# Partial sums of the last block's up stage: kept in PSUM and seeded by ScalarE copies, instead of kept in SBUF and added by VectorE

## The chip, the cores and the metric

The kernel runs as one program on one core of a Trainium2 chip. Its time is the device time of an execution in microseconds (us). The profile is of one execution on the same kind of core; its rows count from the first instruction. PE is TensorE's matmul pipeline, PEld its weight loads, DVE is VectorE, ACT is ScalarE, POOL is GpSimd, and SP issues most of the DMAs.

## What is computed

One layer of a hybrid encoder (chunk attention and a matrix memory side by side, then a feed-forward network) is run on 2048 prompt rows and 8 x 16 sample rows. The change lies in the feed-forward part:

```
def conv_ffn(h, buf, w_up, w_conv, b_conv, w_down):
    u = h @ w_up                       # 1024 -> 2 * 2816 columns
    ext = concatenate([buf, u], axis=1)
    y = b_conv
    for j in range(CONV_W):            # width 3, along the rows of time
        y = y + ext[:, j:j + S] * w_conv[j]
    gate, up = split(y, 2, axis=-1)
    return (gelu(gate, approximate=True) * up) @ w_down, ext[:, S:]
```

Everything is float32.

## The kernel before

**Blocks and stages.** The 17 tiles of 128 rows are worked off in three blocks (FBLOCKS). Each block has an up stage (h @ w_up, convolution, gate) and a down stage. The last block (b = 2) holds tiles 12 to 15 and the sample tile; its half is n = 320 columns wide (HALF), and its up stage is what the change touches. The up stage has 22 steps, one for each 128 columns of the gate half and of the up half; in block 2 they go in the order 0, 11, 1, 12, 2, 13, ... (ORDERS).

**Seven products for eight.** In each step, a 2 x 2 product of blocks is formed by a Strassen-Winograd scheme with seven products P1 to P7. The B tiles hold the seven combinations of h, made earlier; the weights hold seven combinations of w_up, four of which (`wsd`) were stored in DRAM by block 0. Each product is four contraction tiles of 128, and each float32 product is made of three fp32r matmuls (mm3, L104 to L106: high by high, low by high, high by low), so a product is 12 matmuls of 320 columns, and a step 84.

**Weights.** load_quads issues a step's weights from SP in two groups, of four quads and of three, each quad 128 x 512 floats (256 KB). load_up splits each into a high part (ACT, L1309) and a low part (DVE, L1310) in one of two `wh`/`wl` buffers or of the four `w3` tiles.

**A step's PSUM and its sums.** `a` (ua, 2 buffers), `d_` (ub, 2 buffers) and `ec` (uec, 2 buffers of two banks: e and c). Before the change a step is:

- P1 into a; ACT copies it to x1 in SBUF (L1617).
- P6 into d_; DVE makes x2 = x1 + d_ (L1619).
- P7 into e; DVE makes x3 = x2 + e (L1621).
- P5 into c; DVE makes the second half of uu = x3 + c, in three pieces of 128, 64 and 128 columns (second, L1483).
- P2 onto a; ACT copies a into the first half of ug (L1640).
- P4 onto e; DVE makes the first half of uu = x2 + e (L1642).
- P3 onto c; DVE makes the second half of ug = x2 + c, three pieces (L1483).

"Onto" means that the matmuls accumulate on what the bank holds. uu and ug rotate through three buffers (u_tile). Then conv runs for uu and for ug: small POOL copies of the two carried rows (L1494 to L1499), a scaled ACT pass (L1502), two DVE passes (L1503, L1504), and for ug the GELU on ACT (L1506). DVE multiplies gate by up (L1652, L1655), forms four combinations every second step (L1595) and POOL stores them.

**Other work in the stage.** Twelve units finish block 1's output beside it (later): SP loads f0d or f1d and x2d, DVE scales (L1431), POOL adds (L1432) and stores.

**What sets the order.** The program is written as a list of operations and a scheduler with a timeline model orders the instructions of each engine when the program is built. That order is then fixed: each engine runs its own list from top to bottom, and an instruction that waits on a semaphore holds up all behind it on its engine.

Of the kernel before, what the change touches and what calls it, by code (L numbers as in the profile page):

```python
# [10 lines left out]
F32 = mybir.dt.float32  # L11
F32R = mybir.dt.float32r
AF = mybir.ActivationFunctionType
ALU = mybir.AluOpType
# [3 lines left out]
P = 128  # L18
# [21 lines left out]
PAIRS = [[(((b[j], 0), (b[j + 3], 0)), j * P, P, f"{b[j]}") for j in range(3)] for b in FBLOCKS[:2]]  # L40
NK = NF // 2
FAST = (1, 2)
ORDERS = [[f for k in range(NK) for f in (k, k + NK)] if b in FAST else list(range(NF)) for b in range(3)]
B11, B12, B22, B21 = range(4)
T1, T3, T2, T4 = range(4, 8)
# [4 lines left out]
def hymba_step(ctx: ExitStack, tc: tile.TileContext, I: dict, O: dict):  # L50
    nc = tc.nc
# [20 lines left out]
    def dt_(shape, name):  # L72
        return dram.tile(shape, F32, tag=name, name=name)
# [28 lines left out]
    def mm3(out, ah, al, bh, bl, start, stop, onto=False):  # L102

        nc.tensor.matmul(out, ah, bh, start=start, stop=False, skip_group_check=onto)  # L104
        nc.tensor.matmul(out, ah, bl, start=False, stop=False, skip_group_check=onto)  # L105
        nc.tensor.matmul(out, al, bh, start=False, stop=stop, skip_group_check=onto)  # L106
# [938 lines left out]
    P1, P6, P7, P5, P2, P4, P3 = range(7)  # L1045
# [13 lines left out]
    def quad(name):  # L1059
        return ffn.p3.tile([P, 512], F32, tag="q", name=name, bufs=11)  # L1060
# [184 lines left out]
    for n_, (half, gi) in enumerate(seq):  # L1245
        wh, wl, _ = pend
# [4 lines left out]
        g = GROUPS[gi]  # L1251
        i = int(g[2])
        nm = f"{g}_{half}"
# [60 lines left out]
    def load_quads(b, f, g):  # L1314

        src = lambda i: I["w_up"][f][:, i * 512:(i + 1) * 512]
        if b == 0 and g == 0:
            q = []
            for i in range(4):
                q.append(quad(f"wu{f}_{i}"))  # L1320
                nc.sync.dma_start(q[i], src(i))
            a11, a12, a22, a21 = q
            s1, s2, s3, s4 = [quad(f"ws{f}_{i}") for i in range(4)]
            for o, x, y, op in ((s1, a21, a22, ALU.add), (s2, s1, a11, ALU.subtract), (s3, a11, a21, ALU.subtract),
                                (s4, a12, s2, ALU.subtract)):
                nc.vector.tensor_tensor(o, x, y, op=op)
            for i, o in enumerate((s2, s3, s1, s4)):
                nc.gpsimd.dma_start(wsd[f][:, i * 512:(i + 1) * 512], o)
            raws[f] = [a12, a22, s4]
            return [a11, s2, s3, s1]  # L1330
        if b == 0:
            return raws.pop(f)
        kept = lambda i: wsd[f][:, i * 512:(i + 1) * 512]
        out = []
        for i, s_ in enumerate([[src(0), kept(0), kept(1), kept(2)], [src(1), src(2), kept(3)]][g]):
            r = quad(f"wu{b}_{f}_{g}_{i}")
            nc.sync.dma_start(r, s_)
            out.append(r)
        return out

    def load_up(b, i, g, quads=None):
        f = ORDERS[b][i]
        n = 2 * i + g
# [102 lines left out]
    p4 = ffn.p4 = ctx.enter_context(tc.tile_pool(name="p4", bufs=1, side="right", reuse_waits="tile"))  # L1446
# [13 lines left out]
    def u_tile(name):  # L1460
        turns[0] += 1
        if turns[0] % 3:
            return rows_tile("xr", [P, D], name)[:, :770]
        return p4.tile([P, 770], F32, tag="u", name=name)

    for b, tiles in enumerate(FBLOCKS):
        last = b == len(FBLOCKS) - 1
        fast = b in FAST
        nt = len(tiles)
        n = HALF[b]  # L1470
# [4 lines left out]
        def product(i, w, acc, onto=False):  # L1475
            for k in range(4):
                c = slice(k * P, (k + 1) * P)
                mm3(acc[:, :n], w[0][:, c], w[1][:, c], B[i][:, 0, k, :n], B[i][:, 1, k, :n],
                    start=not onto and k == 0, stop=k == 3, onto=onto)

        def second(u, x, acc):

            add = lambda o, c, v=lambda t: t: nc.vector.tensor_tensor(o, v(x[:, c]), v(acc[:, c]), op=ALU.add)  # L1483
            if not last:
                add(u[:, 2 + n:2 + 2 * n], slice(0, n))
                return
            add(u[:, 2 + n + 64:2 + n + 192], slice(0, P))
            add(u[:, 2 + n:2 + n + 64], slice(2 * P, n))
            us = u[:, 2 + npr:2 + ln].rearrange("p (b s) -> p b s", b=DB)
            add(us[:, :, 2:DS + 2], slice(P, 2 * P), lambda t: t.rearrange("p (b s) -> p b s", b=DB))  # L1490
# [24 lines left out]
        g, parts = {}, {}  # L1515
# [84 lines left out]
        unfinished = []  # L1600
        for fi, f in enumerate(ORDERS[b]):
            w = pend.pop(0)
            ahead_of(2 * fi + 2)
            if fi >= 3:
                next(done, None)
            if fi == NF - 2:
                for i in range(2):
                    if fast:
                        fetch_a(i)
                    else:  # L1610
                        fetch(0, i, True)
            nm = f"{b}_{f}"
            a, d_, ec = ps_mm(f"ua{nm}"), ps_sm(f"ub{nm}"), ps_big(f"uec{nm}")
            e, c = ec[:, 0:512], ec[:, 512:1024]
            x1, x2, x3 = [p4.tile([P, 384], F32, tag="x", name=f"x{i}_{nm}", bufs=3) for i in range(3)]
            product(P1, w[0], a)
            nc.scalar.copy(x1[:, :n], a[:, :n])  # L1617
            product(P6, w[1], d_)
            nc.vector.tensor_tensor(x2[:, :n], x1[:, :n], d_[:, :n], op=ALU.add)  # L1619
            product(P7, w[2], e)  # L1620
            nc.vector.tensor_tensor(x3[:, :n], x2[:, :n], e[:, :n], op=ALU.add)  # L1621
            product(P5, w[3], c)
            uu = u_tile(f"uu{nm}")
            second(uu, x3, c)
            w = pend.pop(0)
            ahead_of(2 * fi + 3)
            if fi == NF - 1:
                if fast:
                    split_a(0)
                    split_a(1)  # L1630
                    for i in range(2, 5):
                        fetch_a(i)
                else:
                    split_g(0, 0, w3_tile)
                    split_g(0, 1, w3_tile)
                    for k in range(2, 5):
                        fetch(0, k, True)
            ug = u_tile(f"ug{nm}")
            product(P2, w[0], a, onto=True)
            nc.scalar.copy(ug[:, 2:2 + n], a[:, :n])  # L1640
            product(P4, w[1], e, onto=True)
            nc.vector.tensor_tensor(uu[:, 2:2 + n], x2[:, :n], e[:, :n], op=ALU.add)  # L1642
            product(P3, w[2], c, onto=True)
            second(ug, x2, c)
# [21 lines left out]
        if fast:  # L1666
# [73 lines left out]
            kept = {}  # L1740
# [22 lines left out]
            for p, (_, _, set_, onto) in enumerate(SEQUENCE):  # L1763
                for c in range(3):
# [19 lines left out]
                    for k in range(4 * c, min(4 * c + 4, NK)):  # L1784
                        i = 6 * p + k // 2
# [198 lines left out]
```

## Time and profile before

| what | value |
|---|---|
| runs of the kernel | 2768.33, 2776.52, 2780.66 us; median 2776.52 |
| profiled execution | 2780.55 us, its span 2778.8 us, 1.75 us outside the span |
| granted TensorE clock | 0.994 of full, mean |
| last block's up stage | 2338.5 to 2634.5 us of the span, 296 us |
| PE instructions in that stretch | 1890 matmuls (1848 of the stage, the rest of the neighbouring down stages) |

The stretch begins where the first `ua` matmul of 320 columns stands in the timeline (2338.5 us) and ends with the last `uec` matmul (2634.1 us). Busy times overlap a little where instructions are pipelined: a matmul of 320 columns is shown as 0.31 us long, while one starts every 0.147 us. For a busy PE the count of matmuls in a stretch therefore tells more than the busy time.

### The profile page before, as it was taken

What the parts mean: (1) busy time and instruction counts of PE and PEld (TensorE: products, weight loads), DVE (VectorE), ACT (ScalarE), POOL (GpSimd) and SP (SyncE); (2) the same over time, 40 slices, a digit from 0 to 9 for tenths busy, and PEclk for the clock granted to TensorE, in tenths of its full rate; (3) what the DMA queues carried; (4) which work ended last, traced back from release to release, by engine and by line L of the source; (5) the groups of instructions that cost most, each with busy time, mean ns of one, the idle gap of its engine ahead of it and who ended that gap; (6) DMA issues with size and microseconds to landing.
All of it is one profiled execution on the core that took longest, in us unless ns stands there. A gap on an engine that the chain in (4) does not pass through costs nothing.

```text
span 2778.8 us, 47788 instructions
## 1 busy us (share of the span) xinstructions
PE 2700.5 (97%) x16422; PEld 2525.1 (91%) x16422; DVE 1971.7 (71%) x3637; ACT 1439.6 (52%) x2918; POOL 658.6 (24%) x1249
## 2 busy tenths in 40 slices
PE   7999999999999999999999999999999999999998
PEld 7899999998899998878999998789999778989976
DVE  5244455645546668766989987668998866999966
ACT  4355555634346666543555455445455665545554
POOL 1000010211100002335433322123442112555301
PEclk9999999999999999999999999999999999999999
DMA  5534355556564456345645559866775766777775
GB/s 182 157 116 139 105 164 168 163 152 211 156 184 141 136 169 196 107 163 195 230 153 188 167 183 329 301 224 198 225 225 170 250 223 231 216 236 231 233 268 183
DMA packets 322850, 532.52 MB, mean 192 GB/s; under 512 B 59650, under 2 KB 156638, under 8 KB 322478
## 3 DMA queue, kind: packets, MB, share of 16 engines
q1 hardware_dynamic: 251838, 400.11, 46.6%
q0 software_dynamic: 25840, 83.98, 7.9%
q10 hardware_dynamic: 44928, 45.37, 5.0%
q8 instruction: 129, 2.11, 0.3%
q14 instruction: 115, 0.94, 0.1%
HBM read 383.28 MB, written 149.18 MB: 192 GB/s over the span
## 4 chain that ended last, share of the span: by engine, by line
PE 49%; DVE 5%; DMA 3%; issue 2%; ACT 1%; POOL 1%; SPq 0%; DVEq 0%; POOLq 0%; ACTq 0%
PE uec L104 5%; PE uec L105 5%; PE uec L106 5%; PE dn L106 4%; PE dn L105 3%; PE dn L104 3%; PE ua L106 3%; PE ua L105 3%; PE ua L104 3%; PE wo L106 2%; PE wo L104 2%; PE wo L105 2%; PE dnm L105 1%; PE dnm L106 1%; PE dnm L104 1%
## 5 line engine op out<-in xcount | busy, mean ns | idle before, releaser
L104 PE MATMUL uec<-B,wuh 128*128 128x384 f32 (+1 forms) x720 | 237.8, 331 | 11.8 <-DVE uu L1642 10.7
L105 PE MATMUL uec<-B,wuh 128*128 128x384 f32 (+1 forms) x720 | 236.5, 328 | 0.0
L106 PE MATMUL uec<-B,wul 128*128 128x384 f32 (+1 forms) x720 | 234.8, 328 | 0.0
L1309 ACT CAST wuh<-wu 128x512 fp32r<-128x512 f32 x255 | 141.4, 618 | 112.4 <-PE uec L105 105.4
L1310 DVE TENSOR_TENSOR wul<-wu,wuh 128x512 fp32r<-128x512 f32 x255 | 170.4, 703 | 4.0 <-DMA x2d<-mx 2.8
L405 DVE CUSTOM_DVE_ANT_0 tmp<-s,nb 128x640 f32<-128x640 f32 (+4 forms) x128 | 94.4, 738 | 95.6 <-PE s L395 94.2
L104 PE MATMUL vo<-wi_h,hT 128*128 128x256 f32 x544 | 155.2, 285 | 0.8 <-DVE mt L211 0.6
L106 PE MATMUL vo<-wi_h,hT 128*128 128x256 f32 x544 | 155.6, 286 | 0.0
L105 PE MATMUL vo<-wi_l,hT 128*128 128x256 f32 x544 | 154.8, 285 | 0.0
L104 PEld LDWEIGHTS uec<-B,wuh 128*128 128x128 f32 x720 | 136.2, 189 | 15.3 <-DVE uu L1642 12.4
L104 PE MATMUL qk<-hT,wi_h 128*128 128x384 f32 (+1 forms) x384 | 130.3, 339 | 7.4 <-ACT qk_st L236 4.1
L105 PEld LDWEIGHTS uec<-B,wuh 128*128 128x128 f32 x720 | 136.4, 189 | 0.2
L106 PEld LDWEIGHTS uec<-B,wul 128*128 128x128 f32 x720 | 136.2, 189 | 0.0
L1506 ACT ACTIVATE y<-y 128x768 f32<-128x768 f32 (+1 forms) x66 | 53.8, 815 | 155.5 <-DVE y L1504 155.5
L418 DVE TENSOR_TENSOR ptl<-pt,pth 128x640 fp32r<-128x640 f32 (+4 forms) x128 | 93.7, 738 | 56.5 <-ACT pth L417 55.5
L406 ACT ACTIVATE tmp<-tmp,mn 128x640 f32<-128x640 f32 (+4 forms) x128 | 97.6, 762 | 64.2 <-DVE mn L405 62.4
L1310 DVE TENSOR_TENSOR wdl<-wdr,wdh 128x512 fp32r<-128x512 f32 x198 | 124.9, 686 | 7.0 <-ACT wdh L1309 6.8
L105 PE MATMUL qk<-hT,wi_h 128*128 128x384 f32 (+1 forms) x384 | 128.9, 336 | 0.0
L106 PE MATMUL qk<-hT,wi_l 128*128 128x384 f32 (+1 forms) x384 | 128.5, 335 | 0.0
L1310 DVE TENSOR_TENSOR al<-ar,ah 128x768 fp32r<-128x768 f32 (+2 forms) x94 | 71.1, 765 | 80.9 <-ACT ah L1309 80.7
L105 PE MATMUL qb<-hT,wi_h 128*128 128x384 f32 (+1 forms) x384 | 127.9, 333 | 0.0
L106 PE MATMUL qb<-hT,wi_l 128*128 128x384 f32 (+1 forms) x384 | 127.2, 331 | 0.0
(443 smaller groups left out, 9443.9 us busy)
## 6 DMA issues: line engine op xcount, KB each, us to landing
wu<-in_w_up SPq DMA_DIRECT2D x220, 256.0 KB, 4.4
wu<-wsd SPq DMA_DIRECT2D x176, 256.0 KB, 4.1
wdr<-in_w_down SPq DMA_DIRECT2D x110, 256.0 KB, 5.8
wi_raw<-in_w_in SPq DMA_DIRECT2D x52, 512.0 KB, 4.0
wsd<-ws POOLq DMA_DIRECT2D x88, 256.0 KB, 3.7
wdr<-wtd SPq DMA_DIRECT2D x88, 256.0 KB, 4.8
gr<-gd SPq DMA_DIRECT2D x39, 384.0 KB, 5.9
kraw<-kTd SPq DMA_DIRECT2D x112, 128.0 KB, 3.2
```

The costliest lines, as they stand in the source:

```text
L104: nc.tensor.matmul(out, ah, bh, start=start, stop=False, skip_group_check=onto)
L105: nc.tensor.matmul(out, ah, bl, start=False, stop=False, skip_group_check=onto)
L106: nc.tensor.matmul(out, al, bh, start=False, stop=stop, skip_group_check=onto)
L405: nc.vector.tensor_tensor_reduce(o_, s_, b_, 1.0, 3e38, ALU.add, ALU.min, accum_out=mn)
L406: nc.scalar.activation(tmp[:, :n], tmp[:, :n], AF.Exp, bias=mn, scale=-1.0, accum_out=rsum[:, i % 4, hh:hh + 1])
L418: nc.vector.tensor_tensor(s.ptl[:, sl, qc], ptv, s.pth[:, sl, qc], op=ALU.subtract)
L1309: nc.scalar.copy(h, r)
L1310: nc.vector.tensor_tensor(l, r, h, op=ALU.subtract)
L1506: nc.scalar.activation(y[:, :ln], y[:, :ln], AF.Gelu_apprx_tanh)
```

## The change

Only steps of block 2 (SEEDED) are touched; blocks 0 and 1 take the old path. The products of a step now go P1, P7, P6, P2, then P5, P4, P3, and the weights are loaded in that order. The partial sums stay in PSUM: ACT copies a (= P1) into d_, which is now one bank of ec, P6 accumulates onto d_, ACT copies d_ into c, the other bank of ec, and P5, P4 and P3 accumulate onto c, d_ and c. P7 goes into the ub bank and is copied by ACT to SBUF (p7). DVE is left with uu = p7 + c and uu = p7 + d_; the second half of ug is three ACT copies out of c. The buffer for ug is taken before the one for uu.

```diff
+SEEDED = (2,)
...
+        groups = [[src(0), kept(0), kept(1), kept(2)], [src(1), src(2), kept(3)]]
+        if b in SEEDED:
+            groups = [[src(0), kept(1), kept(0), src(1)], [kept(2), src(2), kept(3)]]
...
+            def add(o, c, v=lambda t: t):
+                if x is None:
+                    nc.scalar.copy(o, v(acc[:, c]))
+                else:
+                    nc.vector.tensor_tensor(o, v(x[:, c]), v(acc[:, c]), op=ALU.add)
...
+            a, sm_, ec = ps_mm(f"ua{nm}"), ps_sm(f"ub{nm}"), ps_big(f"uec{nm}")
+            seeded = b in SEEDED
+            xs = [p4.tile([P, 384], F32, tag="x", name=f"x{i}_{nm}", bufs=3) for i in range(1 if seeded else 3)]
+            if seeded:
+                d_, c, e, p7 = ec[:, 0:512], ec[:, 512:1024], sm_, xs[0]
+                product(P1, w[0], a)
+                nc.scalar.copy(d_[:, :n], a[:, :n])
+                product(P7, w[1], e)
+                nc.scalar.copy(p7[:, :n], e[:, :n])
+                product(P6, w[2], d_, onto=True)
+                nc.scalar.copy(c[:, :n], d_[:, :n])
+                product(P2, w[3], a, onto=True)
+                ug, uu = u_tile(f"ug{nm}"), u_tile(f"uu{nm}")
+                nc.scalar.copy(ug[:, 2:2 + n], a[:, :n])
...
+            if seeded:
+                product(P5, w[0], c, onto=True)
+                second(uu, p7, c)
+                product(P4, w[1], d_, onto=True)
+                nc.vector.tensor_tensor(uu[:, 2:2 + n], p7[:, :n], d_[:, :n], op=ALU.add)
+                product(P3, w[2], c, onto=True)
+                second(ug, None, c)
```

The scheduler orders the whole stage anew. Up to the stage the order on every engine is as before. In the rows below, the number behind a tile's name is its step (x_2_4, uec_4: step 4), behind it stands the buffer; uec is d_ and c, ub is P7's bank, wuh/wul are weight parts, y_f_0 belongs to ug and y_f_1 to uu.

On ACT, around step 4, before:

```order
L1502 ACTIVATE y_3_0_27622<-ug_3_27568,wcv 128x656
L1309 CAST wu_4_1_1_27719<-wu_4_1_2_27726 128x512
L1640 COPY ug_14_27734<-ua_14_27657 128x320
L1617 COPY x_2_4_27839<-ua_4_27836 128x320
L1506 ACTIVATE y_3_0_27622<-y_3_0_27622 128x656
L1502 ACTIVATE y_14_1_27780<-uu_14_27714,wcv 128x656
L1309 CAST wuh_15_0_27811<-wu_15_0_0_27813 128x512
```

And on ACT at the same place in the changed kernel (its lines are 1 to 11 higher there):

```order
L1511 ACTIVATE y_3_0_27608<-ug_3_27536,wcv 128x656
L1628 COPY uec_4_27822<-ua_4_27820 128x320
L1630 COPY x_2_4_27823<-ub_4_27821 128x320
L1515 ACTIVATE y_3_0_27608<-y_3_0_27608 128x656
L1632 COPY uec_4_27822<-uec_4_27822 128x320
L1310 CAST wuh_15_0_27795<-wu_15_0_0_27797 128x512
L1310 CAST wuh_15_0_27795<-wu_15_0_1_27799 128x512
L1310 CAST wuh_15_0_27795<-wu_15_0_2_27801 128x512
L1310 CAST wuh_15_0_27795<-wu_15_0_3_27803 128x512
L1635 COPY ug_4_27875<-ua_4_27820 128x320
```

The one copy x1 has become three: the seed of d_ (L1628), the copy of P7 (L1630) and the seed of c (L1632), with step 3's GELU (L1515) ahead of the last of them.

On DVE, around the same steps, before:

```order
L1503 SCALAR_TENSOR_TENSOR y_3_0_27622<-ug_3_27568,wcv,y_3_0_27622 128x656
L1310 TENSOR_TENSOR wu_4_1_3_27721<-wu_4_1_2_27726,wu_4_1_1_27719 128x512
L1619 TENSOR_TENSOR x_2_4_27840<-x_2_4_27839,ub_4_27837 128x320
L1504 SCALAR_TENSOR_TENSOR y_3_0_27622<-ug_3_27568,wcv,y_3_0_27622 128x656
L1621 TENSOR_TENSOR x_2_4_27841<-x_2_4_27840,uec_4_27838 128x320
L1652 TENSOR_TENSOR g_3_27627<-y_3_0_27622,y_3_1_27614 128x2x256
L1655 TENSOR_TENSOR g_3_27627<-y_3_0_27622,y_3_1_27614 128x128
L1595 TENSOR_TENSOR s_2_3_27799<-g_3_27627 128x256
L1642 TENSOR_TENSOR uu_14_27714<-x_2_14_27661,uec_14_27659 128x320
```

And on DVE in the changed kernel:

```order
L1512 SCALAR_TENSOR_TENSOR y_3_0_27608<-ug_3_27536,wcv,y_3_0_27608 128x656
L1513 SCALAR_TENSOR_TENSOR y_3_0_27608<-ug_3_27536,wcv,y_3_0_27608 128x656
L1491 TENSOR_TENSOR uu_14_27699<-x_2_14_27646,uec_14_27645 128x128
L1491 TENSOR_TENSOR uu_14_27699<-x_2_14_27646,uec_14_27645 128x64
L1491 TENSOR_TENSOR uu_14_27699<-x_2_14_27646,uec_14_27645 128x8x16
L1683 TENSOR_TENSOR g_3_27613<-y_3_0_27608,y_3_1_27600 128x2x256
L1686 TENSOR_TENSOR g_3_27613<-y_3_0_27608,y_3_1_27600 128x128
L1604 TENSOR_TENSOR s_2_3_27783<-g_3_27613 128x256
L1311 TENSOR_TENSOR wul_15_0_27796<-wu_15_0_0_27797,wuh_15_0_27795 128x512
L1311 TENSOR_TENSOR wul_15_0_27796<-wu_15_0_1_27799,wuh_15_0_27795 128x512
L1311 TENSOR_TENSOR wul_15_0_27796<-wu_15_0_2_27801,wuh_15_0_27795 128x512
L1665 TENSOR_TENSOR uu_14_27699<-x_2_14_27646,uec_14_27645 128x320
```

The sums x2 and x3 between the two passes of y_3_0 are gone, and so are the three sums for ug further down; the two passes stand next to each other. On PE the 84 matmuls of a step are the same in number and size; in step 4 the program has 2 of P1 and 2 of P7, then the other 10 of P1, 10 of P7, 12 of P6 and 12 of P2 in a row, then P4 of step 14 and P5 of step 4.

More of the change, by code (lines that the diff above doesn't have):

```diff
@@ L1334, in load_quads @@
         out = []
-        for i, s_ in enumerate([[src(0), kept(0), kept(1), kept(2)], [src(1), src(2), kept(3)]][g]):
+        groups = [[src(0), kept(0), kept(1), kept(2)], [src(1), src(2), kept(3)]]
+        if b in SEEDED:
+            groups = [[src(0), kept(1), kept(0), src(1)], [kept(2), src(2), kept(3)]]
+        for i, s_ in enumerate(groups[g]):
             r = quad(f"wu{b}_{f}_{g}_{i}")
@@ L1481, in second @@
         def second(u, x, acc):
-            add = lambda o, c, v=lambda t: t: nc.vector.tensor_tensor(o, v(x[:, c]), v(acc[:, c]), op=ALU.add)
+            def add(o, c, v=lambda t: t):
[3 more added lines that the diff above has]
+                    nc.vector.tensor_tensor(o, v(x[:, c]), v(acc[:, c]), op=ALU.add)
             if not last:
@@ L1612, in hymba_step @@
             nm = f"{b}_{f}"
[L1613 to L1624, printed above, removed]
+            a, sm_, ec = ps_mm(f"ua{nm}"), ps_sm(f"ub{nm}"), ps_big(f"uec{nm}")
[12 more added lines that the diff above has]
+                nc.scalar.copy(ug[:, 2:2 + n], a[:, :n])
+            else:
+                d_, e, c = sm_, ec[:, 0:512], ec[:, 512:1024]
+                x1, x2, x3 = xs
+                product(P1, w[0], a)
+                nc.scalar.copy(x1[:, :n], a[:, :n])
+                product(P6, w[1], d_)
+                nc.vector.tensor_tensor(x2[:, :n], x1[:, :n], d_[:, :n], op=ALU.add)
+                product(P7, w[2], e)
+                nc.vector.tensor_tensor(x3[:, :n], x2[:, :n], e[:, :n], op=ALU.add)
+                product(P5, w[3], c)
+                uu = u_tile(f"uu{nm}")
+                second(uu, x3, c)
             w = pend.pop(0)
@@ L1637, in hymba_step @@
                         fetch(0, k, True)
[L1638 to L1644, printed above, removed]
+            if seeded:
[5 more added lines that the diff above has]
+                second(ug, None, c)
+            else:
+                ug = u_tile(f"ug{nm}")
+                product(P2, w[0], a, onto=True)
+                nc.scalar.copy(ug[:, 2:2 + n], a[:, :n])
+                product(P4, w[1], e, onto=True)
+                nc.vector.tensor_tensor(uu[:, 2:2 + n], x2[:, :n], e[:, :n], op=ALU.add)
+                product(P3, w[2], c, onto=True)
+                second(ug, x2, c)
             yu = conv(uu, 1, f)
```

## The prediction

> **What bounds the kernel now.** I read the page's busy shares first, then the stretches of the last block's up stage, then who waited for whom in it, then the PE timeline around the longest wait.
>
> ```profile
> PE 2700.5 (97%) x16422; PEld 2525.1 (91%) x16422; DVE 1971.7 (71%) x3637; ACT 1439.6 (52%) x2918; POOL 658.6 (24%) x1249
> ```
>
> Over the whole span PE is busy 97% and DVE only 71%. That average hides the stage that the change touches:
>
> ```profile
> core 0: us, PE busy (x) PEld busy (x) DVE busy (x) ACT busy (x) POOL busy (x), PEclk, DMA share, GB/s
> 2338.50:2634.50 296.00, 285.88 (x1890) 281.94 (x1888) 269.94 (x539) 158.67 (x280) 149.22 (x296) 0.98 0.70 227
> 2350.00:2400.00 50.00, 50.00 (x343) 50.00 (x342) 44.52 (x93) 29.02 (x50) 18.77 (x42) 1.00 0.60 187
> 2400.00:2450.00 50.00, 47.66 (x320) 46.66 (x319) 46.48 (x94) 24.58 (x42) 31.86 (x55) 1.00 0.77 240
> 2450.00:2500.00 50.00, 45.77 (x298) 45.50 (x297) 46.64 (x89) 25.69 (x46) 29.09 (x53) 0.93 0.69 221
> 2500.00:2550.00 50.00, 48.56 (x332) 48.30 (x331) 49.98 (x99) 27.54 (x48) 28.80 (x57) 1.00 0.75 246
> 2550.00:2600.00 50.00, 47.89 (x317) 47.63 (x316) 46.21 (x97) 25.44 (x44) 24.39 (x53) 0.97 0.61 200
> ```
>
> Here DVE is busy 91%, and in the four later windows 46.2 to 49.98 of 50 us. The count of matmuls tells what this costs. The first window has 343, PE at its densest, with DVE busy 44.52 us: so DVE at 89% did not hold PE up. The next four have 320, 298, 332 and 317, together 105 too few; at 50 / 343 = 0.146 us each, that is **15.3 us lost**. Over the stage, 1848 matmuls at 0.147 us are 271.7 us, the other 42 some 7 us (most are wider), so at most 296 - 278.7 = 17.3 us can be had at all.
>
> ```profile
> PE uec L104 <- DVE uu L1642: 9.7, 4, 4.2
> ACT y L1506 <- DVE y L1504: 57.6, 17, 6.2
> ACT wuh L1309 <- PE uec L105: 25.7, 18, 3.4
> ```
>
> PE waited only for DVE: four times, 9.7 us in all, the longest 4.2. The other 5 us or so are in the clock after two of these waits:
>
> ```profile
> 2471.25 0.31 PE L106 MATMUL ua<-B,wul 128*128 128x320 f32 x1
> 2475.80 0.64 PE L104 MATMUL uec<-B,wuh 128*128 128x320 f32 x1 [4.23 <-DVE uu L1642]
> 2476.23 0.47 PE L105 MATMUL uec<-B,wuh 128*128 128x320 f32 x1
> 2476.50 0.47 PE L106 MATMUL uec<-B,wul 128*128 128x320 f32 x1
> ...
> 2555.88 0.64 PE L104 MATMUL uec<-B,wuh 128*128 128x320 f32 x1 [2.11 <-DVE uu L1642]
> 2556.31 0.47 PE L105 MATMUL uec<-B,wuh 128*128 128x320 f32 x1
> 2556.58 0.47 PE L106 MATMUL uec<-B,wul 128*128 128x320 f32 x1
> ```
>
> After 4.23 us of waiting, and again after 2.11 us, matmuls start 0.27 us apart instead of 0.147; that is the granted clock of 0.93 and 0.97 in these windows. So a wait of 2 us costs more than itself. (The Trainium skill, "TensorE: Matmul & The Clock Gate", section "HAM oscillation — how this bites in real kernels", states the rule that gaps of PE should not exceed some 3.4 us. By it only the 4.23 us gap would have lowered the clock; here 2.11 us did too, so the row decides, and short waits are priced with their slow matmuls behind them.)
>
> **What the change removes.** Three sums of each of the 22 steps leave DVE:
>
> ```profile
> L1483 DVE TENSOR_TENSOR ug<-x,uec 128x128 f32<-128x128 f32 (+1 forms) x66 | 13.5, 259 | 6.8 <-PE uec L106 6.8
> L1621 DVE TENSOR_TENSOR x<-x,uec 128x320 f32<-128x320 f32 x22 | 10.6, 480 | 0.6 <-PE uec L106 0.5
> L1619 DVE TENSOR_TENSOR x<-x,ub 128x320 f32<-128x320 f32 x22 | 10.5, 479 | 0.8 <-PE ub L106 0.7
> ```
>
> That is 13.5 + 10.6 + 10.5 = **34.6 us of DVE**, 5.84 us for each 50 us of the stage. If PE ran dense in the four windows, DVE would need there (46.48 - 5.84) x 343/320 = 43.6, (46.64 - 5.84) x 343/298 = 47.0, (49.98 - 5.84) x 343/332 = 45.6 and (46.21 - 5.84) x 343/317 = 43.7 us of 50. Two are below the 44.52 us at which PE ran dense; two lie 2.5 and 1.1 us above.
>
> **What it adds.** ACT gets the two seeds (d_ from a, c from d_) and three pieces of ug; the copy of P7 takes the place of the old copy x1. The nearest rows:
>
> ```profile
> L1617 ACT COPY x<-ua 128x320 f32<-128x320 f32 x22 | 9.2, 417 | 8.7 <-PE ua L106 8.7
> L236 ACT COPY vo_st<-vo 128x256 f32<-128x256 f32 x68 | 24.9, 367 | 20.6 <-PE vo L106 20.1
> L703 ACT ACTIVATE kw<-ms,colsp 128x128 f32<-128x128 f32 x64 | 23.2, 362 | 23.6 <-PE ms L76 22.3 <-PE qk L106 0.4 <-PE sot L106 0.4
> ```
>
> From 256 to 320 columns a copy grows by 50 ns, 0.78 ns a column, so 128 and 64 columns come to 0.27 and 0.22 us; the three pieces are 0.76 us, at most 1.09 by the third row. No row shows ACT writing PSUM; I take 0.417 us for a seed, the same length from PSUM to SBUF, with 0.36 and 0.62 us (the split's 512-column pass on ACT, below) as ends. A step adds 2 x 0.417 + 0.76 = 1.6 us, the stage 35 us: ACT goes from 158.7 to 194 us of some 280, 69%, at the upper ends 76%. It has the room; what counts is when its copies run. (The Trainium skill, "ScalarE: Activation LUTs", section "What ACT_TABLE_LOAD costs", gives 186 ns + 0.833 ns per column, 0.45 us for 320: an estimate that would add 1.5 us of ACT to the stage and leave the forecast where it is. Its remark that ScalarE writes PSUM faster than SBUF no run here shows yet.)
>
> **The new waits of PE.** P6 now waits for the seed of d_, P5 for the seed of c. Before, P6 and P5 began in banks of their own and waited for no partial sum of their step. The seed of d_ has the least cover: in the order around step 4, ten matmuls of P7 stand between the last of P1 and the first of P6, 1.47 us. The hand-over is small in these rows:
>
> ```profile
> 2399.91 0.31 PE L106 MATMUL ua<-B,wul 128*128 128x320 f32 x1
> 2400.26 0.43 ACT L1617 COPY x<-ua 128x320 f32<-128x320 f32 x1 [1.12 <-PE ua L106]
> ```
>
> The matmul ends at 2400.22 and the copy starts at 2400.26. From the start of P1's last matmul: 0.31 + 0.04 + 0.42 + 0.05 back to PE = 0.82 us, while P6 is due after 11 x 0.147 = 1.62. **0.8 us is spare.** The instruction just ahead on ACT is the scaled pass of the step before, which is 0.93 us long:
>
> ```profile
> L1502 ACT ACTIVATE y<-ug,wcv 128x656 f32<-128x656 f32 x21 | 19.6, 931 | 1.0 <-DVE ug L1483 1.0
> L1309 ACT CAST wuh<-wu 128x512 fp32r<-128x512 f32 x98 | 53.6, 618 | 27.3 <-PE uec L105 25.7 <-issue 1.3
> ```
>
> If such a pass (or a split's, 0.62 us) has just begun when P1 ends, the seed is at most 0.2 us late; 22 steps make 0 to 5 us. I take 1.2, since ACT is idle for a third of the time. The seed of c has P2 as cover, 1.76 us, or more where products of the other step stand between; queued ahead of it stands the GELU, which waits for DVE. With DVE relieved I let it cost nothing here; the price if not is rival 2. Behind a late GELU queue the seed, the high parts of the next weights (each needed by PE and then by DVE) and the copy of ug.
>
> DVE's own lateness I set at 1.8 us, half of the 2.5 + 1.1 us that two windows need above the proven 44.52; it lies between 0 (DVE did run at 49.98 with 332 matmuls) and 3.6. The SP loads are as many and as large as before, only in another order: nothing, hidden behind DVE and PE, since waits for transfers in the stage come to 1.7 us:
>
> ```profile
> DVE f L1431 <- DMA f<-f1d: 1.7, 2, 1.4
> ```
>
> These stay. POOL's copies are the same in number.
>
> **The sum.** 15.3 - 1.2 - 1.8 = 12.3 us off the profiled execution's 2780.55, which gives 2768.2. That execution lies 4.0 us above the median of the runs shown, 2776.52; against the median the forecast is **2764 us**. It is a shortening by 0.45%. About 0.5%, 13.9 us, is what a measurement of this kernel can tell from no change.
>
> **Rivals.**
>
> 1. *Nothing stays late.* The seeds are always in time and the transition into the down stage gains as well: up to 17.3 us, 2759 us. For it: 89% of DVE was enough in the first window. Against it: two windows will need more than that.
>
> 2. *ACT becomes the bound, through the GELU* (slower). In the rows above ACT stood 17 times before L1506 for DVE's second pass, 57.6 us, 3.4 us on the mean, and nothing on PE hung on that. Now the seed of c is behind it. If DVE's passes come as late as before, P2's 1.76 us cover is overrun by 1.6 us a step, 22 x 1.6 = 36 us, and 36 - 15.3 = 21 us more than before: 2797 us, more with the slow clock. It decides from an overrun of (15.3 + 13.9) / 22 = 1.3 us a step. Against it: those waits arose with DVE at 93% and more; DVE now has 9% in reserve, and in step 4 P4 of step 14 stands between as well, 3.5 us of cover.
>
> 3. *Half is lost again.* The waits for seeds and POOL's stretching of DVE (the row of 1.64 us below, twelve times) eat half the gain: 2769 to 2776 us.
>
> ```profile
> L1432 POOL TENSOR_TENSOR f<-f,x 128x512 f32<-128x512 f32 x12 | 19.7, 1646 | 11.6 <-DVE f L1431 8.5 <-DVE wul L1310 3.1
> ```
>
> **How the numbers follow.** Forecast (8 to 16 us gained): 0.55, of which 0.20 lies beyond 13.9 us. Rival 1: 0.20. Rival 3: 0.11. Rival 2: 0.14, of which 0.12 beyond 13.9 us. So faster by over 0.5% 0.40, within 0.5% 0.48, slower 0.12. The range goes from rival 1 less 5 us, because runs of one kernel spread from 8 us below to 4 above their median, to 2784, which takes in rival 3, no gain with that spread, and the start of rival 2; the rest of rival 2 is left out.
>
> **What would show it.** Right: the five windows hold 335 to 343 matmuls each, DVE is near 44 of 50 us, ACT near 33, no wait of PE for DVE above 1 us, the stage some 283 us long. Wrong: P6 or P5 (uec) waiting for ACT in the list of waits, with the GELU's own wait for DVE still above 40 us in total: rival 2 or 3. If the seeds run above 0.62 us, their price was wrong. If the counts reach 343 and the time does not fall, the stage's end is given back in the down stage.

## The result: 0.2% slower, and the profile after

The changed kernel took **2782.02 us** (median of 20 runs, 2775.03 to 2788.42); the kernel before, run beside it, 2776.93 us (2768.33 to 2789.21). The ratio is 1.0020, with a 95% interval from 1.0012 to 1.0029: 5 us slower, where 12 us less had been forecast. The interval leaves out 1, but the difference is under the 0.5% that the prediction took as the least to be told from no change. The profiled execution of the changed kernel took 2781.67 us, its span is 2780.0 us.

The busy shares of the changed kernel first:

```profile
PE 2700.0 (97%) x16422; PEld 2520.6 (91%) x16422; DVE 1948.4 (70%) x3527; ACT 1463.7 (53%) x3028; POOL 669.8 (24%) x1249
```

PE did the same matmuls. DVE lost its 110 instructions and ACT gained 110. But DVE's busy time fell by 23.3 us, not by 34.6, and ACT's rose by 24.1, not by 35. Now the last block's up stage, cut as it was for the kernel before (start, end, then length, and busy time with the count of instructions for PE, PEld, DVE, ACT and POOL, then the granted clock):

```profile
2332.50:2633.50 301.00, 288.49 (x1892) 278.72 (x1891) 245.65 (x430) 182.41 (x386) 156.48 (x296) 1.00 0.69 224
2350.00:2400.00 50.00, 47.71 (x317) 46.18 (x316) 38.45 (x67) 30.02 (x64) 21.12 (x41) 1.00 0.54 173
2400.00:2450.00 50.00, 48.27 (x324) 47.16 (x323) 44.84 (x79) 28.84 (x59) 32.28 (x56) 1.00 0.79 249
2450.00:2500.00 50.00, 47.69 (x319) 46.33 (x318) 45.17 (x75) 33.44 (x73) 30.90 (x57) 1.00 0.77 244
2500.00:2550.00 50.00, 48.27 (x324) 47.14 (x323) 44.13 (x76) 29.86 (x63) 30.24 (x56) 1.00 0.71 222
2550.00:2600.00 50.00, 47.58 (x316) 45.99 (x315) 41.26 (x77) 30.74 (x64) 24.22 (x51) 1.00 0.62 201
```

The stage takes 301 us instead of 296. (The two spans differ by only 1.2 us, since the stage began 6 us earlier in this execution. The order up to the stage is the same in both kernels, so those 6 us are no effect of the change.) No window is dense any more: 316 to 324 matmuls in each, also in the first, which held 343 before. And DVE is busy only 38 to 45 us in them, in three of the five less than the 44.5 us at which PE had run dense. Something is lost in small pieces all along the stage. The list of PE's waits in the stage (what waited and for whom, then us in total, times, longest) names it:

```profile
PE uec L105 <- DVE uu L1665: 7.5, 13, 0.7
PE ua L105 <- ACT wuh L1310: 3.9, 7, 0.6
PE dn L106 <- DVE wdl L1311: 1.1, 1, 1.1
```

Four long waits have become twenty short ones and one for a weight of the down stage, and **none of them is for a seed**. Thirteen times PE waits for DVE's add out of d_ (L1665), seven times for the high part of a weight. One of each kind, from the timelines of the changed kernel:

```profile
2431.46 0.30 PE L107 MATMUL uec<-B,wul 128*128 128x320 f32 x1
2431.81 0.49 DVE L1665 TENSOR_TENSOR uu<-x,uec 128x320 f32<-128x320 f32 x1 [1.26 <-PE uec L107]
2432.35 0.41 PE L105 MATMUL uec<-B,wuh 128*128 128x320 f32 x1 [0.58 <-DVE uu L1665]
2432.60 0.31 PE L106 MATMUL uec<-B,wuh 128*128 128x320 f32 x1
...
2433.92 0.31 PE L106 MATMUL uec<-B,wuh 128*128 128x320 f32 x1
2434.07 0.31 PE L107 MATMUL uec<-B,wul 128*128 128x320 f32 x1
2434.27 1.66 ACT L1310 CAST wuh<-wu 128x512 fp32r<-128x512 f32 x3 [0.94 <-DMA f<-f0d]
2434.94 0.41 PE L105 MATMUL ua<-B,wuh 128*128 128x320 f32 x1 [0.56 <-ACT wuh L1310]
2435.19 0.31 PE L106 MATMUL ua<-B,wuh 128*128 128x320 f32 x1
```

The matmul at 2431.46 is the last of P4, onto d_; the one at 2432.35 the first of P3, onto c. DVE stands ready (it had waited 1.26 us for P4 itself) and starts its read 0.04 us after P4 ends; P3 starts 0.05 us after the read ends. So nobody is late here: the 0.89 us from start to start, where 0.147 would do, is the hand-over P4 to DVE to P3 itself, and no relief of DVE can shorten it. The second place is alike. P3's last reader of the weights' high part (L106) ends at 2434.23, ACT's conversion for the next step starts at 2434.27, and P1, which stands directly behind P3, waits for it. (The view puts ACT's own wait here down to a DMA; ACT started 0.04 us after the matmul, and eleven other waits of such conversions, 31.5 us in all, are put down to PE's L106.)

So why does P3, which writes c, wait for a read of d_? d_ and c are the two banks of one tile, `ec`, and the built program keeps dependencies by tile: by the semaphores of step 8, P4's first matmul waits for DVE's last read of c and P3's first for L1665. Both exist in the kernel before too, where P4 and P3 write e and c. What is new is the distance. In the order of the built kernel before, 10 to 48 other matmuls stand between the last of P4 and the first of P3 in all 22 steps; the four steps with only 10 are the four with the long waits for L1642. In the changed one there are none in **12** steps and a single one in another; these are the 13 waits.

Start-to-start distances above 0.147 us per matmul, added up over the stage's timeline, give what this costs: 19.8 us in the changed kernel, 10.8 of them right behind the 13 waits for L1665 and 7.8 behind the seven for a weight. In the kernel before it is 15.0 us, 14.0 behind the four waits for L1642. The 4.8 us more agree with the 5 us between the medians. They need not be all of it: in the down stage behind, PE's named waits are 5.6 us in the changed kernel's profile and 3.9 us before.

### The profile page after: what moved, and what is told of

The parts are those of the page before. It is cut to its first block, busy times and chain, and to the rows that moved or that the text cites. A ratio compares the mean times of both kernels' runs of the same rounds, so it can differ in the third digit from the quotient of the medians.

```text
span 2780.0 us, 47719 instructions
## 1 busy us (share of the span) xinstructions
PE 2700.0 (97%) x16422; PEld 2520.6 (91%) x16422; DVE 1948.4 (70%) x3527; ACT 1463.7 (53%) x3028; POOL 669.8 (24%) x1249
## 3 DMA queue, kind: packets, MB, share of 16 engines
q8 instruction: 129, 2.11, 0.3%
## 4 chain that ended last, share of the span: by engine, by line
PE 50%; DVE 4%; DMA 3%; issue 2%; ACT 1%; POOL 1%; SPq 0%; DVEq 0%; POOLq 0%; ACTq 0%
PE uec L105 6%; PE uec L106 5%; PE uec L107 5%; PE dn L107 4%; PE dn L106 3%; PE dn L105 3%; PE ua L105 3%; PE ua L107 3%; PE ua L106 3%; PE dnm L106 2%; PE dnm L107 2%; PE ub L105 1%; PE dnm L105 1%; PE wo L105 1%; PE wo L107 1%
## 5 line engine op out<-in xcount | busy, mean ns | idle before, releaser
L106 PE MATMUL uec<-B,wuh 128*128 128x384 f32 (+1 forms) x720 | 235.2, 327 | 0.0
L1311 DVE TENSOR_TENSOR wul<-wu,wuh 128x512 fp32r<-128x512 f32 x255 | 167.5, 694 | 18.7 <-ACT wuh L1310 15.6
L106 PE MATMUL vo<-wi_l,hT 128*128 128x256 f32 x544 | 154.8, 284 | 0.0
L106 PEld LDWEIGHTS uec<-B,wuh 128*128 128x128 f32 x720 | 135.2, 188 | 0.2
L1311 DVE TENSOR_TENSOR wdl<-wdr,wdh 128x512 fp32r<-128x512 f32 x198 | 125.2, 685 | 7.7 <-ACT wdh L1310 6.5
L1311 DVE TENSOR_TENSOR al<-ar,ah 128x768 fp32r<-128x768 f32 (+2 forms) x94 | 71.0, 764 | 82.2 <-ACT ah L1310 80.8
L105 PE MATMUL dn<-wdh,ah 128*128 128x512 f32 x308 | 122.1, 396 | 6.0 <-ACT ah L1310 6.0
L106 PE MATMUL qb<-hT,wi_h 128*128 128x384 f32 (+1 forms) x384 | 127.9, 333 | 0.0
L106 PE MATMUL qk<-hT,wi_h 128*128 128x384 f32 (+1 forms) x384 | 127.8, 333 | 0.0
```

Of the source, the lines that this page charges most:

```text
L1311: nc.vector.tensor_tensor(l, r, h, op=ALU.subtract)
```

## Experiments

**Theory A**: the shared tile, with P4 and P3 back to back, and P1 back to back with P3 over a weight buffer, costs TensorE the time. **Theory B**, the one that the prediction rests on: the load of VectorE (or, after the change, of ScalarE with its seeds) holds the stage. The times of the kernel before differ from batch to batch (2776.7 to 2780.6 us), so each result goes by its ratio to the runs beside it. The scheduler orders the stage anew after each of these edits, so that a run differs from its neighbour by its order too.

### The other place for d_

```diff
-                d_, c, e, p7 = ec[:, 0:512], ec[:, 512:1024], sm_, xs[0]
+                d_, c, e, p7 = sm_, ec[:, 512:1024], ec[:, 0:512], xs[0]
```

> The changed kernel with one edit: d_ takes P1+P6 in the ub bank, and P7 shares the two-bank tile with c. Theory A (P3 onto c is held up because DVE's read of d_, L1665, is in the other bank of the same tile, and the order has P3 directly behind P4 in 13 steps): the 13 waits of PE for L1665, 7.5 us, go, with the slow matmuls behind them about 11 us, so some 2771 us, 0.2% under the kernel before; PE's 7 waits for ACT's wuh remain if the order still puts P1 behind the product that frees its buffer. Theory B (ScalarE's added 35 us and the seeds hold the stage up): nothing changes for ACT, so 2782 us within 3.

Measured: 2768.69 us, ratio 0.9956 (0.9938 to 0.9974). In the first two steps a part of the P1 that is copied into d_ is lost here (64 columns, by the argument at the end), so that this much is left out of the result; the work in time is the same. PE waits for nothing in the stage, and windows of this kernel are dense:

```profile
2339.00:2620.00 281.00, 281.00 (x1893) 278.89 (x1892) 244.46 (x430) 181.79 (x386) 147.85 (x296) 1.00 0.74 239
2400.00:2450.00 50.00, 50.00 (x343) 50.00 (x343) 47.42 (x82) 31.88 (x68) 29.74 (x59) 1.00 0.78 251
```

Same seeds, same instructions on DVE and ACT, 20 us less in the stage. The fall is larger than the 0.2% expected, because the waits for the weights went too, although nothing was done about them: the scheduler's order changed with the places, and by the built programs P1 stands directly behind a P3 in none of the steps, where it did in eight. Theory A.

### The weights' places

```diff
-        if n % 3 < 2:
+        if (g == 0 if b == 2 else n % 3 < 2):
```

> The changed kernel with one edit: in the last block the first weight group of each step always goes to the two wh buffers and the second always to the w3 tiles. Theory A (PE also waits at P1, 7 times 0.56 us, because the split of its weights needs the buffer that the P3 just ahead frees): those waits go; the order now has P3 directly behind P4 once instead of 13 times, so most waits for L1665 go as well: stage 301 to about 283 us, 2764 to 2768 us. Theory B: ACT has as much to do and the w3 tiles are held singly, so ACT's splits of the second group come later: 2782 us or more.

Measured: 2787.74 us, ratio 1.0026 (1.0013 to 1.0039), not faster, where 2764 to 2768 us had been expected. Of the named waits a single one for L1665 is left, but others came in their place:

```profile
PE uec L105 <- ACT uec L1628: 7.3, 8, 2.2
PE uec L105 <- ACT y L1515: 3.2, 1, 3.2
PE uec L105 <- DVE uu L1491: 2.9, 3, 1.3
PE uec L105 <- DVE uu L1665: 2.2, 1, 2.2
```

A miss for Theory A's number. Seven of the eight waits put down to L1628 are P6 waiting for the seed of d_, up to 2.2 us (the eighth is a P4): this is the prediction's late seed, which occurs in this order and not in that of the change. So with a new order a term can't be taken away without moving others.

Both edits together:

> Both edits. Theory A: neither wait is left, PE dense in the stage (335 to 343 matmuls in 50 us), about 279 to 282 us of stage, 2762 to 2765 us, 0.5% under the kernel before. Theory B: 2782 us.

Measured: 2763.31 us, ratio 0.9937 (0.9918 to 0.9956), with 0.5 us of waits for a seed in the stage (the same part of P1 is left out). That is 0.6% under the kernel before, where Theory A had 0.5%; its interval overlaps that of the first edit alone.

### VectorE relieved in the kernel before

The last block leaves out the sum x3, and ScalarE copies the second half of ug, so that P7 and x2 are missing from parts of the result (the new `add`, as in the change, is not shown):

```diff
-            nc.vector.tensor_tensor(x3[:, :n], x2[:, :n], e[:, :n], op=ALU.add)
+            if last:
+                x3 = x2
+            else:
+                nc.vector.tensor_tensor(x3[:, :n], x2[:, :n], e[:, :n], op=ALU.add)
...
-            second(ug, x2, c)
+            second(ug, None if last else x2, c)
```

> The kernel before, with some 24 us of DVE work left out in the last block and the order of products kept: x3's sum is not made (P7 is left out of the second half of uu) and the second half of ug is copied by ACT out of c (x2 is left out of it). It asks what DVE's load alone cost. If the 15 us lost before came from DVE's load: PE's waits fall from 10 us to under 3, DVE near 43 of 50 us, 2764 to 2768 us. If they came from where the scheduler put P3 (behind the read of the other bank), whatever DVE's load: PE still waits some 8 us or more for L1642's place, 2773 to 2780 us.

Measured: 2768.69 us, ratio 0.9959 (0.9944 to 0.9974). In windows of this kernel:

```profile
2342.40:2622.60 280.20, 279.88 (x1886) 277.51 (x1885) 250.28 (x451) 167.44 (x339) 151.14 (x296) 1.00 0.74 239
2400.00:2450.00 50.00, 50.00 (x344) 50.00 (x343) 48.13 (x84) 30.70 (x63) 32.57 (x61) 1.00 0.76 248
```

With less work for DVE the stage regains what it had lost, as Theory B has it. But the run can't tell load from order: in the built program at least 24 matmuls now stand between P4 and P3 in every step, where the four steps that waited had 10. And x3 is also a read of the shared tile, so that the run takes away a possible wait together with the load. That PE is dense with DVE busy 48.13 us of 50 speaks against the load as such.

### The places alone

The kernel before with d_ and e exchanged in the last block, nothing else:

```diff
             e, c = ec[:, 0:512], ec[:, 512:1024]
+            if last:
+                d_, e = e, d_
```

> The kernel before, with d_ and e exchanged in the last block alone: no seed, no operation less, VectorE's work of 270 us in the stage as it was. It tells what the kernel before loses its 15 us by. If by the shared tile (c and e in one tile, so that P5, P4 and P3 wait for reads of the other bank), the stage takes 282 to 287 us and the median falls by 9 to 14 us. If by VectorE's load, which the prediction held, the stage stays at 294 to 298 us and the median within 3 us of the kernel before. About half would mean that both have a part.

Measured: 2771.72 us, ratio 0.9974 (0.9964 to 0.9984), 7 us less. Its windows:

```profile
2350.00:2400.00 50.00, 50.00 (x344) 50.00 (x343) 46.02 (x93) 28.41 (x48) 20.10 (x46) 1.00 0.64 208
2400.00:2450.00 50.00, 50.00 (x344) 50.00 (x342) 49.59 (x100) 28.01 (x48) 32.95 (x54) 1.00 0.77 244
2450.00:2500.00 50.00, 49.88 (x341) 49.62 (x340) 49.20 (x98) 28.21 (x48) 35.01 (x58) 1.00 0.76 252
2500.00:2550.00 50.00, 48.60 (x332) 48.27 (x331) 48.79 (x98) 26.19 (x45) 27.90 (x54) 1.00 0.78 241
2550.00:2600.00 50.00, 50.00 (x343) 50.00 (x343) 48.32 (x103) 29.71 (x51) 27.18 (x53) 1.00 0.64 203
```

One wait of PE is left in the stage, then stands the first one of the down stage:

```profile
PE uec L104 <- DVE x L1621: 1.4, 1, 1.4
```

```profile
PE dn L104 <- ACT ah L1309: 6.9, 1, 6.9
```

DVE keeps all its sums, is busy 46 to 49.6 us of 50, and PE runs at 332 to 344 matmuls; what PE loses in the stage falls from 15.0 to 1.6 us. So DVE's load was not a bound by itself. It took late reads of DVE and the shared tile, which makes P3 wait for them. In the built program P3 now waits for DVE's read of c alone, and no P3 stands waiting in the trace, though in four steps only 1 to 5 matmuls stand between P4 and it. The 1.4 us that are left are of the old kind: P5, onto c, waits for DVE's read of d_, which now shares c's tile. The median falls by 7 us, short of the 9 to 14 expected and less than the 13.4 us that the stage gains, since the down stage now waits once for its first high part, 6.9 us (last experiment).

### A longer read

L1665 made in four pieces of 80 columns:

```diff
-                nc.vector.tensor_tensor(uu[:, 2:2 + n], p7[:, :n], d_[:, :n], op=ALU.add)
+                for q in range(0, n, n // 4):
+                    h = slice(q, q + n // 4)
+                    nc.vector.tensor_tensor(uu[:, 2 + h.start:2 + h.stop], p7[:, h], d_[:, h], op=ALU.add)
```

> The changed kernel, with VectorE's add out of d_ (320 columns, 0.49 us) made in four pieces of 80 columns, each some 0.2 us: the read of d_ ends some 0.3 to 0.4 us later, and VectorE has 6 to 9 us more in the stage. Nothing is left out. Theory A: P3 follows P4 without a matmul between them in 12 steps and waits for the last piece, so each of these waits grows from 0.58 us by 0.3 to 0.4: TensorE's waits for uu from 7.5 us to 11 to 13, the stage 3 to 6 us longer than with the change, the median 3 to 6 us above it. Theory B (VectorE's load as such): the waits for uu stay at 0.5 to 0.7 us each, and what is lost is spread over other releasers.

Measured: 2787.57 us, ratio 1.0031 (1.0018 to 1.0044). PE's waits in the stage:

```profile
PE uec L105 <- DVE uu L1667: 9.1, 12, 0.8
PE ua L105 <- ACT wuh L1310: 3.9, 7, 0.6
PE uec L105 <- ACT uec L1632: 1.4, 2, 1.1
```

The pieces have L1667 here. The 12 waits are again those of P3 where at most one matmul stands between P4 and it, each now 0.76 us on the mean instead of 0.58. The direction and the place are Theory A's, and the stage is 4 us longer, as expected; the size of a wait grew by half of what was expected (0.18 us, not 0.3 to 0.4), because the four pieces overlap: together they take 0.67 us where the one add took 0.49. The total of 9.1 us lies below the 11 to 13 expected.

### ug's pieces back on VectorE

```diff
-                    nc.scalar.copy(o, v(acc[:, c]))
+                    nc.vector.tensor_copy(o, v(acc[:, c]))
```

> The changed kernel, with the three pieces of ug copied by VectorE in place of ScalarE: VectorE's work in the stage rises by some 13 us, to about 259, ScalarE's falls by 16 us. The places in PSUM stay as they are, and nothing is left out. P3 follows P4 directly in 10 steps instead of 13. Theory A (the shared tile): the waits of P3 for uu stay at about 0.6 to 0.7 us each, 6 to 8 us in all, and the stage stays at 297 to 304 us; the median within 4 us of the changed kernel. Theory B (the load of ScalarE, or that of VectorE, holds the stage): with ScalarE's load, the stage falls below 295 us; with VectorE's, it rises above 306 us.

Measured: 2790.25 us, ratio 1.0047 (1.0035 to 1.0058). The stage takes 308 us. PE's waits in it:

```profile
PE uec L105 <- DVE uu L1665: 5.2, 9, 0.6
PE ua L105 <- ACT wuh L1310: 3.9, 7, 0.6
PE ua L107 <- DVE wul L1311: 3.3, 7, 0.5
```

Taking work off ScalarE does not help, so its load is not the bound. But the expectation of Theory A is missed: the median is some 8 us above that of the change, and the stage passes the 306 us that were put down for VectorE's load. Most of the stage's 7 us more are no lost time, though: it holds 1912 matmuls in place of 1892, 20 of the down stage more, at 0.23 us each. The waits for L1665 did not grow, 0.58 us each in 9 places. But where P1 already waits for ACT's conversion, DVE's low part (L1311) now comes late as well, 3.3 us in all; and the first wait of the down stage is 6.2 us long, where it was 3.8. So more load on DVE can cost where PE has no distance to the instruction it waits for; how much of the 8 us that is, this run does not settle.

### Seeds and places together

The changed kernel with the exchange from its third step on, in the last block alone (the first two steps keep their places, so that all columns of d_ get their P1):

```diff
-                d_, c, e, p7 = ec[:, 0:512], ec[:, 512:1024], sm_, xs[0]
+                d_, c, e, p7 = sm_, ec[:, 512:1024], ec[:, 0:512], xs[0]
+                if fi < 2:
+                    d_, e = e, d_
```

> The changed kernel, with d_ and e exchanged from the third step on: d_ lies in the single-bank tile and e beside c in the two-bank tile, so that P3 (onto c) no longer waits for VectorE's read of d_, nor P4 (onto d_) for the read of c. The first two steps keep the places of the changed kernel. Nothing is left out. Theory A (the shared tile, with P4 and P3 back to back, costs TensorE some 10 to 20 us): the stage in 280 to 283 us, 335 to 344 matmuls in every window of 50 us, TensorE waiting for the uu reads for under 1 us in all, the median 10 to 14 us under the kernel before. Theory B (the load of VectorE and ScalarE holds the stage, whatever the places): the stage stays at 296 to 301 us and the median within 4 us of the kernel before.

Measured: 2768.20 us, ratio 0.9965 (0.9952 to 0.9977). From 2400 to 2600 us each window holds 343 or 344 matmuls, with DVE at 43 to 48 us; what PE loses in the stage is 1.6 us. The first window, which holds the two steps with the old places, has 328. The stage is 282 us long and the median 10.7 us under the kernel before. But for that first window these are Theory A's numbers.

The same with the weights' places of the second experiment:

> The previous kernel with the weights' ScalarE conversions placed in the first group of a step alone. Nothing is left out. Theory A: the waits of P1 for a weight's conversion go as well, but with the places right they were short already, so 2 to 6 us less than the previous kernel, 14 to 18 us under the kernel before. Theory B: as the kernel before, within 4 us, or slower, since ScalarE's work then lies in front of the seeds.

Measured: 2771.47 us, ratio 0.9974 (0.9963 to 0.9985): no gain, against the expectation. PE waits five times for the seed of d_ (1.7 us), twice for a low part (1.9 us) and once for DVE's read of c (2.0 us).

The kernel before with the exchange in all three blocks:

> The kernel before, with d_ and e exchanged in all three blocks rather than in the last alone. Nothing is left out. In the first two blocks of the kernel before TensorE waited for the uu reads twice, 1.0 us in all, so by Theory A there is little to be had there: 0 to 2 us less than with the exchange in the last block alone, 7 to 9 us below the kernel before. A fall of over 4 us more would mean that the shared tile also costs time where no wait names it.

Measured: 2766.39 us, ratio 0.9959 (0.9945 to 0.9974), 10.6 us under the kernel before where 7 to 9 had been expected; the interval overlaps that of the exchange in the last block alone. Last, on one chip, the same once more and the changed kernel with the exchange in all three blocks:

```diff
-                d_, e, c = sm_, ec[:, 0:512], ec[:, 512:1024]
+                d_, e, c = ec[:, 0:512], sm_, ec[:, 512:1024]
```

> The kernel before with d_ and e exchanged in all three blocks, once more, as the companion of the kernel with seeds. Nothing is left out. 8 to 13 us under the kernel before, ratio 0.995 to 0.997.

> The changed kernel with d_ and e exchanged in all three blocks (in the seeded stage from its third step on): seeds and right places together. Nothing is left out. With the kernel that has the exchange alone, beside it on the same chip, it tells what the seeds are worth once no wait is made by the shared tile. If VectorE's relief is worth something then (part of the forecast's 12.3 us), it is 3 us or more faster than the exchange alone; if TensorE was dense already without it, the two are within 3 us of each other, both 8 to 14 us under the kernel before.

Measured: the exchange alone 2764.24 us, ratio 0.9956 (0.9941 to 0.9971); seeds and exchange **2759.80 us**, ratio 0.9946 (0.9926 to 0.9967). Both beat the two kernels of this study. The second has the lowest median, 17 us under the kernel before and 4.4 us under the exchange alone, more than the 3 us that were to show a worth of the seeds; but its six runs lie from 2754.93 to 2771.45 us and the intervals overlap, so what the seeds add is not settled. Their up stages can't be told apart. From 2400 to 2450 us, first with the exchange alone, then with the seeds too:

```profile
2400.00:2450.00 50.00, 50.00 (x343) 50.00 (x342) 49.29 (x96) 27.24 (x48) 32.52 (x55) 1.00 0.79 246
```

```profile
2400.00:2450.00 50.00, 50.00 (x343) 50.00 (x342) 48.07 (x80) 34.17 (x72) 33.28 (x57) 1.00 0.78 258
```

343 matmuls in both. The profile with the seeds is 10.1 us shorter, but 6.8 us of that lie ahead of the stage (it begins at 2324.9 us with the seeds and at 2331.7 without), where both programs have the same order. Behind that they differ where the down stage begins; PE's waits there, in the same order:

```profile
PE dn L104 <- ACT ah L1309: 6.7, 1, 6.7
```

```profile
PE dn L105 <- ACT ah L1310: 3.0, 1, 3.0
```

When the up stage ends earlier, PE reaches the down stage before its first operand is converted. DVE and ACT have the gate and the combinations of the last step to finish first, and with the seeds PE's wait for them is 3.7 us shorter, by these two profiles. The seeds' part of the gain, if it is real, would lie there and not in the stage that they were put in. That was read from one profile each and not tried by itself.

## Why the prediction was wrong

**What bounds the kernel: right in size, wrong in cause.** The 15.3 us lost in the stage stand (15.0 by the timeline), and several kernels got them back. But "PE waited only for DVE" was read as "DVE is too busy". The row of 4.23 us named L1642, a read of e, as the releaser of P3, which writes c. That a product waits for a read of the other bank should have raised the question what it waits for, before the load of DVE did. The exchange alone showed it: dense at 49.59 us of DVE's 50. The bar of 44.52 us, from which the term of 1.8 us for DVE's lateness was made, is none.

**The failed step: the new waits of PE.** Only the seeds were treated there, P6 for d_ and P5 for c. Not one wait for a seed appears in the changed kernel. The waits that came are P3 behind P4, over the shared tile, 10.8 us, and P1 behind P3, over the weight's buffer, 7.8 us. They were priced at nothing, though that P4 and P3 stand next to each other is to be read from the order of the built program, and the hand-over from rows of the trace: P4's end to DVE 0.04 us, the add 0.49, back to PE 0.05. So the old loss did not simply go. The four long waits, 14.0 of the 15.0 us, are gone; but what P3 waits for is still the read of the other bank, and it came back as 13 short waits. With these 10.8 us, the 7.8 us, and 1.3 us behind a weight of the down stage, PE loses 19.8 us where the prediction had 3.0 (1.2 for seeds and 1.8 for DVE). The measured 2782 us does lie below 2784, the upper end of the range, but that end was made for rivals that did not come, so it is no support.

**DVE's relief and ACT's load.** The durations of the added rows were right:

```profile
L1489 ACT COPY ug<-uec 128x128 f32<-128x128 f32 (+1 forms) x63 | 11.3, 250 | 0.0
L1628 ACT COPY uec<-ua 128x320 f32<-128x320 f32 x22 | 9.6, 436 | 0.0
L1630 ACT COPY x<-ub 128x320 f32<-128x320 f32 x22 | 9.5, 432 | 7.0 <-PE ub L107 7.0
L1632 ACT COPY uec<-uec 128x320 f32<-128x320 f32 x22 | 9.4, 426 | 3.4 <-PE uec L107 3.4
```

A seed takes 436 and 426 ns, where 417 was taken. (The remark of the Trainium skill, "ScalarE: Activation LUTs", section "Step-by-step: what each stage is for", that ScalarE writes PSUM faster than SBUF is not borne out for this form: the copy into SBUF, L1630, takes 432 ns.) Too large was what the sums of these durations were used for. 34.6 and 35 us are sums of shown durations, but instructions that follow each other overlap. Three rows of DVE, in the kernel before:

```profile
2473.66 0.68 DVE L1310 TENSOR_TENSOR wu<-wu,wu 128x512 fp32r<-128x512 f32 x1
2474.26 0.47 DVE L1619 TENSOR_TENSOR x<-x,ub 128x320 f32<-128x320 f32 x1
2474.66 0.68 DVE L1310 TENSOR_TENSOR wu<-wu,wu 128x512 fp32r<-128x512 f32 x1
```

x2 shows 0.47 us and the next starts after 0.40. Over 110 instructions 0.07 us each are some 8 of the 11.3 us between 34.6 and the 23.3 us by which DVE's busy time fell; the rest was not taken apart.

**The rivals.** Rival 2, ACT through the GELU, did not come. The GELU's waits for DVE in the stage, 57.6 us before, are now:

```profile
ACT y L1515 <- DVE y L1513: 8.9, 11, 1.6
```

This is what the argument expected of DVE's relief, though the order around the GELU is new as well. Rival 3, half the gain lost to seeds and POOL, did not come either. No rival had PE wait, within a step, for a read that it does not need; that is the mechanism that put the time on the slower side.

**What would show it.** The list did half its work: counts of 316 to 324 instead of 335 to 343, with DVE at 38 to 45 us and no wait for DVE's sums above 0.7 us, say at once that much of the load is gone and something else is there. It had no sign for what that was.

## What to carry to other kernels

Before an engine's load is called the bound, ask of the releasing instruction whether the waiting one needs its result; where it only touches another bank of the same tile, put the two in separate tiles first, which here was one or two lines and worth 7 to 12 us. When a change moves products, look up in the built order, for every pair with a reader on another engine between them, how many instructions stand in the gap: a gap of none cost the whole hand-over each time here, though DVE stood ready in the place shown. And expect that a stage that ends earlier may give part of it back where the next one begins, as it did here.

## What the runs showed of the hardware

A hand-over PE to DVE to PE over a 320-column add of 0.49 us cost 0.83 us on the mean: 10.8 us in 13 places. Pauses of 0.6 us, twenty of them, left the granted clock of the stage at 1.00. In the kernel before, single ones of 4.23 and 2.11 us stand in windows of 0.93 and 0.97, and the two others, of 1.94 and 1.44 us, in windows of 1.00.

DVE busy 49.6 us of 50 did not hold PE up, with 344 matmuls in the window, where P3 did not wait for the other bank's read.

A value that ScalarE copies into PSUM is not always added to. In the first experiment a part of the seed was lost in the first two steps, the first use of each of two buffers; with these two steps at their old places nothing was. By the program these banks had last been written by transposes of 256 columns, so that 64 of the seed's 320 had not been written then. That the product overwrote these 64 was argued from there, not tried by itself. The Trainium skill, "PSUM — Partial Sum Buffer", section "The four PSUM rules", gives a rule that fits: only TensorE sets the bits that decide between adding and overwriting, and the first matmul of a sum clears them for its whole bank. By it, a bank that is to be seeded must have been written in all the seed's columns by matmuls since it was last cleared.
